# Attention values taken for two query tiles at once, with the column halves' products kept together

## The chip, the cores and the metric

The kernel runs on one core of one Trainium2 chip. The metric is device time in microseconds for one execution of the whole program. Work on a core is done by five engines that run beside each other and meet at semaphores: TensorE (PE; the profile shows its weight loads apart, as PEld), VectorE (DVE), ScalarE (ACT), GpSimd (POOL) and SyncE (SP), which only issues transfers here.

## The reference, cut to what matters

Two layers of a transformer trunk over 512 latent tokens and 256 context tokens, model width 1024, all in fp32. Layer 0 has differential attention (4 heads of width 128) beside neighbourhood attention (8 heads of width 64); layer 1 has windowed attention with 16 query heads of width 64 over 4 key heads. In each the probabilities meet the values at the end, and that product is what the change touches:

```python
# layer 0, differential heads: two softmaxes are subtracted, then times v (width 128)
p = p[:, :, 0] - lam_val * p[:, :, 1]
return jnp.einsum('bhqn,bnhd->bqhd', p.astype(v.dtype), v)
...
# layer 0, neighbourhood heads: keys near the query, and all context keys, in one softmax
return (jnp.einsum('bhcij,bicjhd->bchd', p_nb, v_r)
        + jnp.einsum('bhcn,bnhd->bchd', p_ctx, vcx))
...
# layer 1: a query block of 128 sees the context and the key blocks before, at and after it
band = ... & (jnp.abs(q_pos[:, None] - k_pos[None, :]) <= SWA_WINDOW)
p = jax.nn.softmax(jnp.concatenate([s, sink], axis=-1), axis=-1)[..., :-1]
o = jnp.einsum('bkgqn,bnkd->bqkgd', p.astype(v.dtype), v)
```

Around this stand adaLN-modulated norms, projections with gated residual adds, and a SwiGLU block in each layer.

## The kernel before, in words

Activations lie with features on the partitions and tokens along the free axis, in tiles of 128 features. Most products with weights are made of three fp32r products of split operands (`mm3`, L205 to L210); transposes and the product of probabilities with values are plain fp32.

**A step of attention** handles one tile of 128 queries for one *unit*: one differential head (`diff_steps`, L788), or two heads of width 64 (`na_steps`, L885; `gqa_step`, L1462). A step has two parts. Part `a` makes the scores (L804 and L805, L912 and L914, L1477 and L1479), adds masks and takes the maximum on DVE (L806, L915, L1481), the exponential on ACT (L808, L922, L1486), and normalises on POOL (L782, L926, L1494). Part `b` turns the probabilities on PE, 128 by 128 at a time, into a PSUM tile `t` (L821, L935, L1503, L1511), copies them to SBUF as `pt` (L822 on ACT; L940 on ACT and L938 on DVE; L1507 and L1512 on ACT, L1505 on DVE), multiplies them with the value tiles (L825, L946, L1517), and copies the result out (L826, L949; `split` at L1521, which is L196 on ACT and L197 on DVE). Each context unit has a step of its own (`ca`, `cb`) for its 256 context queries, with products of 256 columns already (L852, L982).

**Column halves.** In units of two heads, the value tile of one head has 64 columns. Head 0 writes PSUM partitions 0 to 63 and head 1 partitions 64 to 127, so each product occupies 64 of the array's 128 columns (the profile prints `128*64`). The loop is over key tiles, and inside it over the two heads.

**Buffers.** `pt` has 3 buffers in layer 0 (`pt_tile`, L785) and 2 in layer 1 (L1499), each for one step (one head of one step in `na_steps`). PSUM tiles `t` take 2 buffers in layer 0 and 3 in layer 1, shared by turned probabilities and products.

**What sets the order.** `run_steps` (L406) writes part `a` of a step, part `b` of the step before, then pieces of other work (projections of the next unit, rows of the adaLN weights, first parts of the output projection). From this the framework's list scheduler makes each engine's fixed order when the kernel is built; it may put an instruction ahead of others whose operands come later, so products of one tile need not stand together. `issue_after` ties an instruction behind another, and `high_priority` puts it ahead of others that are ready.

Of the kernel before, what the change touches and what calls it, by code (L numbers as in the profile page):

```python
# [37 lines left out]
def tile_trunk(  # L38
# [337 lines left out]
    def rope_of(ps, pool, t=None):  # L376
# [7 lines left out]
        return t  # L384

# [209 lines left out]
    with ExitStack() as st:  # L595
# [189 lines left out]
        def pt_tile(n):  # L785
            return ap.tile([P, n, P], F32, tag="pt", name="pt", bufs=3)

        def diff_steps(u):  # L788
# [4 lines left out]
            def x_step(i):  # L793
# [21 lines left out]
                def b():  # L815
                    v = vunits[u // 2]
                    pt = pt_tile(6)
                    for k0, n in ((0, 4), (4, 2)):
                        t = tp((P, 4, P))
                        for k in range(n):  # L820
                            nc.tensor.transpose(t[:, k, :], d["p"][:, (k0 + k) * P : (k0 + k + 1) * P], ident)  # L821
                        nc.scalar.copy(pt[:, k0 : k0 + n, :], t[:, 0:n, :])  # L822
                    o = tp()
                    for k in range(6):
                        nc.tensor.matmul(o[:, 0:P], v[:, k, vc], pt[:, k, :], start=(k == 0), stop=(k == 5))  # L825
                    nc.scalar.copy(at[:, NC + i * P : NC + (i + 1) * P], o[:, 0:P])  # L826
# [58 lines left out]
        def na_steps(u):  # L885
# [5 lines left out]
            def x_step(j):  # L891
# [37 lines left out]
                def b():  # L929
                    v = vunits[u // 2]  # L930
                    pts = []
                    for c in range(2):
                        t = tp((P, 4, P))
                        for k in range(4):
                            nc.tensor.transpose(t[:, k, :], d["p"][c][:, k * P : (k + 1) * P], ident)  # L935
                        pt = pt_tile(4)
                        if c:
                            nc.vector.tensor_copy(pt, t)  # L938
                        else:
                            nc.scalar.copy(pt, t)  # L940
                        pts.append(pt)
                    o = tp()
                    kts = ((2, 5) if j == 0 else (1 + j, 2 + j)) + (0, 1)
                    for k in range(4):
                        for c in range(2):
                            nc.tensor.matmul(  # L946
                                o[64 * c : 64 * c + 64, 0:P], v[:, kts[(k + 2 * c) % 4], hv[c]], pts[c][:, k, :], start=(k == 0), stop=(k == 3)
                            )
                    nc.scalar.copy(at[:, NC + j * P : NC + (j + 1) * P], o[:, 0:P])  # L949
# [15 lines left out]
            def cb():  # L965
                v = vunits[u // 2]
                pts = []
                for c in range(2):
# [4 lines left out]
                    pt = pt_tile(4).rearrange("p (a b) c -> p a (b c)", b=2)  # L973
                    if c:
                        nc.vector.tensor_copy(pt, t)
                    else:
                        nc.scalar.copy(pt, t)
                    pts.append(pt)
                o = tp()
                for k in range(2):  # L980
                    for c in range(2):
# [922 lines left out]
```

## Time and profile before

| what | value |
|---|---|
| median of 3 runs | 1631.01 us (1628.07 to 1631.24) |
| profiled execution, its own time | 1634.54 us |
| its span, first to last instruction | 1632.7 us |
| mean granted TensorE clock | 0.992 |
| TensorE busy | 1569.6 us (96%) |
| VectorE busy | 1255.6 us (77%) |
| ScalarE busy | 747.0 us (46%) |
| GpSimd busy | 267.0 us (16%) |

The program runs in stages one behind the other. By the first and last starts of their lines: differential attention's products with values from 97.7 to 284.7 us (its first scores at 79.7), neighbourhood attention's from 302.9 to 449.5, layer 0's SwiGLU from 557.7, layer 1's attention from 1059.2 (scores) and 1073.6 (products with values) to 1243.4, and layer 1's SwiGLU to the end.

How to read the rows in this document: a timeline row gives the start in us, the length in us, the engine, the line, the operation, `out<-in`, the shape and how many records were merged. A plain fp32 product shows as two MATMUL records for one instruction, a transpose as one. A record's length includes the depth of the array and overlaps its successor, so that the *difference of two starts* is what work costs TensorE.

### The profile page before, as it was taken

The page shows a single profiled execution, that of the slowest core. Times are in us where ns is not written, and L with a number is a line of the kernel's source. Part 1 is how long each engine was busy: PE and PEld are TensorE (multiplying, and loading weights), DVE is VectorE, ACT ScalarE, POOL GpSimd, SP SyncE. Part 2 cuts the span into 40 slices and gives each one's busy share as a digit, 9 for nine tenths or more (in the row PEclk, how much of TensorE's full clock was granted, in tenths as well). Part 3 has the DMA queues.
Part 4 walks back from the last instruction along what each step waited for, and adds up shares of the span by engine and source line. Part 5 has one row for each costly group of instructions (what it writes and reads, how often), then busy time and mean ns, then how long its engine had stood idle before and what let it go on. Part 6 is the DMA issues. An engine that isn't in the chain of part 4 may idle for free.

```text
span 1632.7 us, 26333 instructions
## 1 busy us (share of the span) xinstructions
PE 1569.6 (96%) x10222; PEld 1403.5 (86%) x10222; DVE 1255.6 (77%) x2157; ACT 747.0 (46%) x1324; POOL 267.0 (16%) x311
## 2 busy tenths in 40 slices
PE   5899998998999999999999999999999999999997
PEld 3798887886878899999999998887788899989897
DVE  4757698976688888978899867787665887869686
ACT  4446554555334532432424244456655542524344
POOL 2222222345010000010100011264322000000001
PEclk9999999999999999999999999999999999999999
DMA  9322244544235365576766753311010442323321
GB/s 343 98 57 85 89 149 129 186 139 132 72 109 154 95 183 158 152 197 168 195 180 169 211 134 95 104 53 40 14 40 27 152 132 66 125 82 104 117 78 52
DMA packets 69220, 198.48 MB, mean 122 GB/s; under 512 B 6900, under 2 KB 19348, under 8 KB 69096
## 3 DMA queue, kind: packets, MB, share of 16 engines
q1 hardware_dynamic: 59464, 164.40, 31.7%
q0 software_dynamic: 9056, 31.87, 9.1%
q8 instruction: 81, 1.33, 0.3%
q10 hardware_dynamic: 576, 0.52, 0.1%
q14 instruction: 43, 0.35, 0.1%
HBM read 160.45 MB, written 4.86 MB: 101 GB/s over the span
## 4 chain that ended last, share of the span: by engine, by line
PE 64%; DVE 7%; DMA 4%; issue 2%; ACT 2%; POOL 0%; DVEq 0%; SPq 0%; ACTq 0%; POOLq 0%
PE f L1272 5%; PE f L1274 5%; PE f L1273 5%; PE f L1685 4%; PE f L1684 4%; PE f L1683 4%; PE f L1313 3%; PE f L1314 3%; PE f L1315 3%; PE t L1517 2%; PE lin L207 2%; PE lin L208 2%; PE lin L209 2%; PE f L1737 2%; PE f L1736 2%; PE f L1738 2%
## 5 line engine op out<-in xcount | busy, mean ns | idle before, releaser
L196 ACT ACTIVATE wh<-raw 128x1024 fp32r<-128x1024 f32 (+1 forms) x96 | 92.3, 978 | 233.7 <-DVE raw L507 115.8
L207 PE MATMUL lin<-hb,wh 128*128 128x512 f32 (+1 forms) x456 | 162.8, 358 | 8.2 <-DVE q L372 2.2
L208 PE MATMUL lin<-hb,wh 128*128 128x512 f32 (+1 forms) x456 | 160.3, 352 | 0.5 <-DVE hb L197 0.4
L209 PE MATMUL lin<-hb,wl 128*128 128x512 f32 (+1 forms) x456 | 158.9, 348 | 0.0
L197 DVE TENSOR_TENSOR wl<-raw,wh 128x1024 fp32r<-128x1024 f32 (+1 forms) x96 | 106.8, 1119 | 34.9 <-ACT wh L196 32.9
L269 DVE SCALAR_TENSOR_TENSOR junk<-raw,tables 128x1024 bf16<-128x1024 f32 x80 | 97.7, 1222 | 20.2 <-DMA raw<-in_ada_wT_dram 19.9
L202 POOL DMA_DIRECT2D wl<-raw x39 | 34.1, 873 | 444.1 <-ACT wl L201 393.8
L207 PEld LDWEIGHTS lin<-hb,wh 128*128 128x128 f32 x456 | 86.4, 190 | 23.4 <-issue 4.5
L1313 PE MATMUL f<-g,wh 128*128 128x512 f32 (+1 forms) x304 | 102.8, 339 | 1.2 <-DVE q L1298 0.7
L1314 PE MATMUL f<-g,wh 128*128 128x512 f32 (+1 forms) x304 | 102.7, 339 | 0.0
L1684 PE MATMUL f<-hb,wh 128*128 128x256 f32 x360 | 101.7, 283 | 0.0
L1683 PE MATMUL f<-hb,wh 128*128 128x256 f32 x360 | 101.4, 283 | 0.0
L1685 PE MATMUL f<-hb,wl 128*128 128x256 f32 x360 | 101.2, 283 | 0.0
L1315 PE MATMUL f<-g,wl 128*128 128x256 f32 (+1 forms) x304 | 100.8, 336 | 0.0
L158 ACT CAST wh<-raw 128x1024 fp32r<-128x1024 f32 x61 | 63.9, 1047 | 77.9 <-PE lin L208 24.0
L1272 PE MATMUL f<-hb,wh 128*128 128x384 f32 x288 | 96.4, 335 | 0.9 <-ACT q L1259 0.9
L159 DVE TENSOR_TENSOR wl<-raw,wh 128x1024 fp32r<-128x1024 f32 x61 | 79.8, 1309 | 22.6 <-ACT wh L158 22.4
L208 PEld LDWEIGHTS lin<-hb,wh 128*128 128x128 f32 x456 | 86.7, 190 | 12.2 <-issue 0.9
L1274 PE MATMUL f<-hb,wl 128*128 128x384 f32 x288 | 96.3, 334 | 0.0
L1273 PE MATMUL f<-hb,wh 128*128 128x384 f32 x288 | 96.2, 334 | 0.0
L209 PEld LDWEIGHTS lin<-hb,wl 128*128 128x128 f32 x456 | 86.6, 190 | 10.4 <-issue 0.3
L339 POOL TENSOR_TENSOR ns_a<-ns_a,ns_s 128x256 f32<-128x256 f32 (+1 forms) x16 | 16.2, 1013 | 435.2 <-ACT ns_s L335 435.2
(395 smaller groups left out, 4948.7 us busy)
## 6 DMA issues: line engine op xcount, KB each, us to landing
raw<-in_w_dram SPq DMA_DIRECT2D x132, 512.0 KB, 3.7
raw<-in_ada_wT_dram SPq DMA_DIRECT2D x80, 512.0 KB, 4.2
wl<-raw POOLq DMA_DIRECT2D x39, 512.0 KB, 5.9
raw<-in_w_ab_dram SPq DMA_DIRECT2D x24, 512.0 KB, 4.2
raw<-in_ada_w_dram SPq DMA_DIRECT2D x16, 512.0 KB, 9.5
k<-k SPq DMA_DIRECT2D x16, 384.0 KB, 5.8
raw<-in_w_c_dram SPq DMA_DIRECT2D x12, 512.0 KB, 3.6
nb<-in_na_bias_dram POOLq DMA_DIRECT2D x16, 256.0 KB, 3.6
```

Of the source, the lines that this page charges most:

```text
L207: nc.tensor.matmul(ps, wh(k), xh(k), start=k == 0, stop=False)
L208: nc.tensor.matmul(ps, wh(k), xl(k), start=False, stop=False)
L209: end = nc.tensor.matmul(ps, wl(k), xh(k), start=False, stop=k == n - 1)
L1272: nc.tensor.matmul(ps, wh(k), b[:, 0, :], start=k == 0, stop=False)
L1273: nc.tensor.matmul(ps, wh(k), b[:, 1, :], start=False, stop=False)
L1274: nc.tensor.matmul(ps, wl(k), b[:, 0, :], start=False, stop=k == 3)
L1313: nc.tensor.matmul(ps, hi, g[:, 0, cols[v]], start=first, stop=False)
L1314: nc.tensor.matmul(ps, hi, g[:, 1, cols[v]], start=False, stop=False)
L1315: nc.tensor.matmul(ps, lo, g[:, 0, cols[v]], start=False, stop=last)
L1683: nc.tensor.matmul(ps, wh(k), b[:, 0, :], start=k == 0, stop=False)
L1684: nc.tensor.matmul(ps, wh(k), b[:, 1, :], start=False, stop=False)
L1685: nc.tensor.matmul(ps, wl(k), b[:, 0, :], start=False, stop=k == 3)
```

## The change

1. `diff_steps`: the step of an even query tile only turns its probabilities and copies them into one half of a `pt` of two steps. The step of the odd tile fills the other half and makes six products of 256 columns (two query tiles at once), and one copy of 256 columns out.
2. `na_steps` and `gqa_step`: the same for pairs of query tiles (0, 1) and (2, 3). Key tiles that both tiles see are met in one product of 256 columns, the others in one of 128, which writes only its tile's half of the output.
3. The products of both heads go through the new `values`, which writes them key tile by key tile, head 1 ahead of head 0, and ties each behind the one before with `issue_after` and `high_priority` (`unbroken`). The context steps of `na_steps` go through it too.
4. `pt` has 1 buffer in both layers, of up to 2 x 2 x 4 (layer 0) or 2 x 10 (layer 1) tiles of 128 columns. A norm's scratch tile `ns_h`, which shared the tag `pt`, shares the tag `p` (5 buffers) instead.

```diff
+    def unbroken(products):
+        last = None
+        for f in products:
+            with tc.issue_after(last.ins) if last else nullcontext(), tc.high_priority() if last else nullcontext():
+                last = f()
+
+    def values(o, terms):
+        unbroken([
+            lambda n=n, c=c, v=v, p=p, cols=cols: nc.tensor.matmul(
+                (lambda z: z if len(p(c).shape) == 2 else z.rearrange("p (a n) -> p a n", n=P))(o[64 * c : 64 * c + 64, cols]),
+                v(c), p(c), start=n == 0, stop=n == len(terms) - 1,
+            )
+            for n, (v, p, cols) in enumerate(terms)
+            for c in (1, 0)
+        ])
...
-        def pt_tile(n):
-            return ap.tile([P, n, P], F32, tag="pt", name="pt", bufs=3)
+        def pt_tile(*n):
+            return ap.tile([P, *n, P], F32, tag="pt", name="pt", bufs=1)
...
                 def b():
                     v = vunits[u // 2]
-                    pt = pt_tile(6)
+                    if i % 2 == 0:
+                        turned["d"] = pt_tile(2, 6)
+                    pt = turned["d"]
...
+                    if i % 2 == 0:
+                        return
                     o = tp()
                     for k in range(6):
-                        nc.tensor.matmul(o[:, 0:P], v[:, k, vc], pt[:, k, :], start=(k == 0), stop=(k == 5))
-                    nc.scalar.copy(at[:, NC + i * P : NC + (i + 1) * P], o[:, 0:P])
+                        nc.tensor.matmul(o[:, 0 : 2 * P].rearrange("p (a n) -> p a n", a=2), v[:, k, vc], pt[:, :, k, :], start=(k == 0), stop=(k == 5))
+                    nc.scalar.copy(at[:, NC + (i - 1) * P : NC + (i + 1) * P], o[:, 0 : 2 * P])
...
-                    kts = ((2, 5) if j == 0 else (1 + j, 2 + j)) + (0, 1)
-                    for k in range(4):
-                        for c in range(2):
-                            nc.tensor.matmul(
-                                o[64 * c : 64 * c + 64, 0:P], v[:, kts[(k + 2 * c) % 4], hv[c]], pts[c][:, k, :], start=(k == 0), stop=(k == 3)
-                            )
-                    nc.scalar.copy(at[:, NC + j * P : NC + (j + 1) * P], o[:, 0:P])
+                    values(o, [
+                        term(0, slice(2, 8, 4), both),
+                        term(2 + (j - 2) % 4, 0, slice(0, P)),
+                        term(1 + j, slice(1, 5, 3), both),
+                        term(2 + j, 5, slice(P, 2 * P)),
+                        term(1, slice(3, 8, 4), both),
+                    ])
+                    nc.scalar.copy(at[:, NC + (j - 1) * P : NC + (j + 1) * P], o[:, both])
...
-                for k in range(2):
-                    for c in range(2):
-                        nc.tensor.matmul(o[64 * c : 64 * c + 64, 0:256], v[:, k, hv[c]], pts[c][:, k, :], start=(k == 0), stop=(k == 1))
+                values(o, [(lambda c, k=k: v[:, k, hv[c]], lambda c, k=k: pts[:, c, k, :], slice(0, NC)) for k in range(2)])
...
-            ns_a0=(ap, "at", 2), ns_a1=(ap, "at", 2), ns_s=(ap, "p", 5), ns_h=(ap, "pt", 3),
+            ns_a0=(ap, "at", 2), ns_a1=(ap, "at", 2), ns_s=(ap, "p", 5), ns_h=(ap, "p", 5),
...
-                pt = gp.tile([P, 2, 5, P], F32, tag="pt", name="pt", bufs=2)
+                h = i % 2
+                if h == 0:
+                    turned[0] = gp.tile([P, 2, 10, P], F32, tag="pt", name="pt", bufs=1)
+                pt = turned[0]
...
+                if h == 0:
+                    return
...
-                split(*(z[:, i // 2, P * (i % 2) : P * (i % 2) + P] for z in att(m)), o[:, 0:P])
+                values(o, [
+                    term(0, slice(0, 6, 5), both),
+                    *([term(i, 2, slice(0, P))] if i > 1 else []),
+                    term(1 + i, slice(3, 8, 4), both),
+                    term(2 + i, slice(4, 9, 4), both),
+                    *([term(3 + i, 9, slice(P, 2 * P))] if i < 3 else []),
+                    term(1, slice(1, 7, 5), both),
+                ])
+                split(*(z[:, i // 2, :] for z in att(m)), o[:, both])
```

Over the whole program the instructions of TensorE in the written order go from 9557 to 9333. Only these products differ in number: in the column halves 432 products (416 of 128 columns, 16 of 256) become 256 (64 of 128 columns, 192 of 256), and with full columns 96 of 128 columns become 48 of 256. ACT issues 32 instructions fewer and DVE 16 fewer (the copies out). POOL and SP issue as many as before, and the transfers keep their sizes.

Where it moves instructions, two places on TensorE. Names that begin with `s` are scores, `t<-ident,p` is a turn of probabilities `p`, and `t<-pt` is a product with values. First layer 1's attention. Before, where the products of three steps meet the next steps' scores and turns:

```order
L1503 MATMUL t_10762<-ident_91,p_10693 128x128 x4
L1511 MATMUL t_10768<-ident_91,p_10684 128x128
L1511 MATMUL t_10768<-ident_91,p_10693 128x128
L1517 MATMUL t_10772<-pt_10755,gv_9570 64x128
L1477 MATMUL s_10888<-gk1_9568,gq_10323 128x256
L1477 MATMUL s_10888<-gk2_9569,gq_10323 128x256
L1479 MATMUL s_10888<-gk1_9568,gq_10323 128x384
L1479 MATMUL s_10888<-gk2_9569,gq_10323 128x384
L1517 MATMUL t_10772<-pt_10755,gv_9570 64x128 x7
L1503 MATMUL t_10811<-ident_91,p_10739 128x128 x4
L1517 MATMUL t_10772<-pt_10755,gv_9570 64x128 x2
L1503 MATMUL t_10817<-ident_91,p_10748 128x128 x4
```

The ten products of one step stand in three places: one, seven and two. After the change, a pair of steps in the same stage:

```order
L1542 MATMUL t_10799<-ident_91,p_10741 128x128 x4
L1542 MATMUL t_10805<-ident_91,p_10750 128x128 x4
L1513 MATMUL s_10878<-gk1_9404,gq_10269 128x256
L1513 MATMUL s_10878<-gk2_9405,gq_10269 128x256
L1515 MATMUL s_10878<-gk1_9404,gq_10269 128x384
L1515 MATMUL s_10878<-gk2_9405,gq_10269 128x384
L396 MATMUL t_10811<-pt_10757,gv_9406 64x256 x2
L396 MATMUL t_10811<-pt_10757,gv_9406 64x128 x2
L396 MATMUL t_10811<-pt_10757,gv_9406 64x256 x6
```

Ten products serve two steps and stand in one place, behind the turns of the second step and four score products.

Second, a context step of neighbourhood attention, before:

```order
L972 MATMUL t_3155<-ident_91,pc_2933 128x128 x4
L209 MATMUL lin_3610<-hb7_131,wl_3518 128x256
L982 MATMUL t_3162<-pt_3153,v_1948 64x256
L912 MATMUL s_3415<-k1_2601,q_2603 128x256
L912 MATMUL s_3415<-k2_2602,q_2603 128x256
L914 MATMUL s_3415<-k1_2601,q_2603 128x256
L914 MATMUL s_3415<-k2_2602,q_2603 128x256
L982 MATMUL t_3162<-pt_3160,v_1948 64x256
L982 MATMUL t_3162<-pt_3153,v_1948 64x256
L982 MATMUL t_3162<-pt_3160,v_1948 64x256
```

and the first one after the change:

```order
L209 MATMUL lin_3463<-hb6_130,wl_3401 128x512
L396 MATMUL t_3067<-pt_3054,v_1903 64x256 x4
L964 MATMUL t_3169<-ident_91,p_3047 128x128 x4
```

Its four products stand together, followed at once by the turns of the next step's probabilities. Over the whole order, runs of products in the column halves that stand together number 102 before (64 in layer 1, 38 in neighbourhood attention) and 31 after (18 and 13).

55 lines of the change are left out of this document (31 added, 24 removed).

## The prediction

> **What bounds the kernel now.** I read the page's busy shares first, then the busy time of each engine in the stages that change, then what TensorE waits for there.
>
> ```profile
> span 1632.7 us, 26333 instructions
> PE 1569.6 (96%) x10222; PEld 1403.5 (86%) x10222; DVE 1255.6 (77%) x2157; ACT 747.0 (46%) x1324; POOL 267.0 (16%) x311
> ```
> ```profile
> core 0: us, PE busy (x) PEld busy (x) DVE busy (x) ACT busy (x) POOL busy (x), PEclk, DMA share, GB/s
> 97.00:300.00 203.00, 193.34 (x1325) 176.52 (x1324) 158.07 (x267) 107.42 (x238) 48.54 (x49) 0.98 0.35 106
> 300.00:350.00 50.00, 50.00 (x357) 42.06 (x355) 44.81 (x82) 23.98 (x54) 22.15 (x28) 1.00 0.63 192
> 300.00:450.00 150.00, 144.10 (x1007) 117.97 (x1006) 104.55 (x188) 72.70 (x168) 53.63 (x78) 0.99 0.43 128
> 1067.00:1245.00 178.00, 174.33 (x1344) 138.93 (x1343) 124.24 (x298) 107.54 (x288) 69.40 (x76) 1.00 0.10 31
> ```
> ```profile
> PE t L1517 <- DVE pt L1505: 1.6, 3, 0.8
> PE s L1477 <- ACT p L1486: 1.2, 2, 0.7
> PE t L1517 <- ACT pt L1507: 0.3, 1, 0.3
> ```
>
> The three stages of the windows are differential attention (97 to 300), neighbourhood attention (300 to 450, its first third shown apart) and layer 1's attention (1067 to 1245). In the last, TensorE is idle for 3.7 of 178 us, DVE for 54 and ACT for 70; the longest waits of TensorE on other engines (the wait rows: total, times, longest) come to 3.1 us. In neighbourhood attention it is idle for 5.9 of 150. So TensorE sets the pace in both, at a granted clock of 0.99 to 1.00, and less of its time there means a shorter span. But busy time includes time in which the array passes nothing, and the timeline shows where:
>
> ```profile
> 1152.01 0.60 PE L1503 MATMUL t<-ident,p 128*128 128x128 f32 x4
> 1152.37 0.48 PE L1477 MATMUL s<-gk,gq 128*128 128x256 f32 x2
> ...
> 1157.00 0.51 PE L1479 MATMUL s<-gk,gq 128*128 128x384 f32 x2
> 1157.35 0.38 PE L1511 MATMUL t<-ident,p 128*128 128x128 f32 x2
> 1157.71 1.09 PE L1517 MATMUL t<-pt,gv 128*64 128x128 f32 x16
> 1158.74 0.66 PE L1503 MATMUL t<-ident,p 128*128 128x128 f32 x4
> 1159.15 0.48 PE L1477 MATMUL s<-gk,gq 128*128 128x256 f32 x2
> 1159.46 0.52 PE L1479 MATMUL s<-gk,gq 128*128 128x384 f32 x2
> 1159.91 0.44 PE L1517 MATMUL t<-pt,gv 128*64 128x128 f32 x4
> 1160.28 0.66 PE L1503 MATMUL t<-ident,p 128*128 128x128 f32 x4
> 1160.69 0.48 PE L1477 MATMUL s<-gk,gq 128*128 128x256 f32 x2
> 1161.01 0.52 PE L1479 MATMUL s<-gk,gq 128*128 128x384 f32 x2
> 1161.46 0.43 PE L1517 MATMUL t<-pt,gv 128*64 128x128 f32 x2
> 1161.82 0.66 PE L1503 MATMUL t<-ident,p 128*128 128x128 f32 x4
> 1162.41 1.09 PE L1517 MATMUL t<-pt,gv 128*64 128x128 f32 x14
> 1163.42 0.66 PE L1503 MATMUL t<-ident,p 128*128 128x128 f32 x4
> ```
>
> Call a run of column-half products that stand together a *visit*. I take differences of starts. The visit of 16 records lasts 1.03 us until the next start, that of 4 records 0.37. The 12 records more cost 0.66; two records, one of each half, run side by side, so this is six steps of **0.11 us**. That leaves 0.37 - 2 x 0.11 = 0.15 us in a visit that is no streaming. Ahead of it, the two L1479 records take 0.45 (1161.01 to 1161.46) against 0.35 where a turn follows (1157.00 to 1157.35): 0.10 more. Behind it, four turns and the next take 0.41 (1158.74 to 1159.15) against 0.36 elsewhere (1152.01 to 1152.37): 0.05 more. **A visit costs 0.30 us beside its products.**
>
> The visit of 2 records, one product of one head alone, lasts 0.36: as much as a pair. That of 14 lasts 1.01, nearly the 1.03 of 16. A product without its partner costs a whole pair's time.
>
> **The change part by part.** *Visits.* TensorE's written order has 102 visits before, 64 in layer 1 and 38 in neighbourhood attention, and 31 after, 18 and 13. 71 fewer at 0.30 us are 21.3 us.
>
> *Steps.* I count two steps of 0.11 for each pair of products, and for a product alone too. Layer 1 before has visits of 1, 7, 2, 8 and 10 products (17, 17, 15, 14, 1 of them): 34 + 136 + 30 + 112 + 10 = 322 steps, 35.4 us. After, each of 16 pairs of query tiles has four pairs of products of 256 columns and one of 128. For 256 columns there is a row, with rows of full columns beside it:
>
> ```profile
> 399.16 1.08 PE L982 MATMUL t<-pt,v 128*64 128x256 f32 x8
> 400.18 0.62 PE L207 MATMUL lin<-hb,wh 128*128 128x512 f32 x2
> ...
> 206.45 1.50 PE L825 MATMUL t<-pt,v 128*128 128x128 f32 x12
> 207.79 0.60 PE L821 MATMUL t<-ident,p 128*128 128x128 f32 x4
> ...
> 188.79 1.03 PE L852 MATMUL t<-pt,v 128*128 128x256 f32 x4
> 189.47 0.47 PE L401 MATMUL lin<-wl,hb 128*128 128x256 f32 x1
> ```
>
> Eight records in 1.02 us, less 0.15, are four steps of **0.22**: twice the columns, twice the time. So 16 x (8 x 0.22 + 2 x 0.11) = 31.7 us, and 0.4 for the one visit of a lone product that is left: 3.3 us saved. Neighbourhood attention before: visits of 1, 7, 8, 4 and 3 products (14, 13, 2, 1, 1) are 156 steps, 17.2 us; its context visits (three of 1, three of 3, one of 4) 22 steps of 0.22, 4.8 us. After: 8 x (6 x 0.22 + 4 x 0.11) + 0.4 + 16 x 0.22 = 18.0 us: 4.0 us saved.
>
> *Full columns.* 12 records take 1.34 us, 0.112 each. The 96 records of 256 columns that replace 192 cost between 0.17 (0.68 over four, L852) and 0.224 each, a gain between 5 and 0 us. I take 0.5, since the column halves show time in proportion to columns. TensorE sheds 21.3 + 3.3 + 4.0 + 0.5 = **29.1 us**.
>
> *What comes back.* The products of a pair now wait for the last copy of its second step; before, the first product began behind the first copy, and scores filled the gap. Queued behind the waiting product on TensorE are the next turns and scores, and DVE's maxima and ACT's exponentials wait for these.
>
> ```profile
> L1505 DVE COPY pt<-t 128x512 f32<-128x512 f32 x32 | 22.0, 687 | 11.7 <-PE t L1503 11.6
> L1507 ACT COPY pt<-t 128x512 f32<-128x512 f32 x32 | 18.7, 583 | 7.4 <-PE t L1503 7.1
> L1517 PEld LDWEIGHTS t<-pt,gv 128*64 128x64 f32 x576 | 34.0, 136 | 16.8 <-issue 6.2 <-DVE pt L1505 3.0 <-ACT es L1488 1.4
> L949 ACT COPY at<-t 128x128 f32<-128x128 f32 x16 | 4.3, 266 | 19.6 <-PE t L946 19.3
> ```
>
> The cover in the new order is typically four score products, two lines of two records; such a group takes 0.77 us (1160.69 to 1161.46). Four turns that start 0.11 apart end 0.66 after the first start, so the last ends 0.33 after its own; with DVE's copy its probabilities are there 1.02 us after that start, and the cover has run out after 0.11 + 0.77 = 0.88. So 0.14 us stays bare at least, more where the copy queues. The bounds are 0 a visit, where more stands between, and a whole copy, 0.69, at each of 28 (31 less three broken ones): 0 to 19 us. I take an estimate of 0.25 a visit, **7 us**, nearest the group row. The present 1.9 us of such waits are not credited against it.
>
> *The rest costs nothing.* DVE and ACT issue 16 and 32 copies out fewer (266 ns each, L949), for wider ones, off TensorE's path. A result that waits for its pair is needed a stage later by the output projection; the last pair of the stage alone has no cover, the 1.02 us above, which lies within the bounds. `ns_h` in the five buffers of `p` is covered by the norm's own chain of DVE and ACT; if not, each of eight tiles would wait one DVE instruction. POOL's and SP's queues issue what they did.
>
> *The sum.* 1634.54 (the profiled execution) - 29.1 + 7 = 1612.4 us, a span near 1610.6. The median shown stands at 1631.01 / 1634.54 = 0.9978 of that execution: **1609 us**.
>
> **A rule weighed.** The Trainium skill, "TensorEngine Tiling (Array Packing)", section "PSUM Bottleneck", says that tiling speeds up TensorE but not the emptying of PSUM, so that the copies may become the bound. In this trace DVE works 70% and ACT 60% of layer 1's attention, which leaves room. By the rule the third rival below would hold. The skill's "TensorE: Matmul & The Clock Gate", section "Back-to-back issue gap", gives about 81 ns for a sustained matmul of 128 columns and 131 for 512, which speaks for the second rival; L982 does not agree.
>
> **The rivals.**
>
> *Nothing comes back.* Scores and fillers cover every copy. Then 1605.4 profiled, 1602. For it: waits of only 1.9 us on `pt` now. Against: the cover must now outlast one full copy.
>
> *Weight loads set the step.* If a step were bound by its load (136 ns a record, two per 0.11 us, in the PEld row) and not by its columns, 256 columns would cost 0.136, not 0.22. 16 x 8 + 8 x 6 = 176 new steps would save 14.8 us more than the forecast: 1594. Against: eight records of L982 in 1.02 us.
>
> *The copies become the bound.* DVE's 124.2 us in the last window must fit in some 161 and its 104.6 in about 139: 77% and 75%, and it is at 90% from 300 to 350 us. If each of the 28 visits waits for a whole copy, 19.3 us come back: 1624.7 profiled, **1621**.
>
> *One buffer of `pt` stops the pipeline (slower).* A refill's first copy must wait for the last product that reads the buffer; with two `t` tiles in layer 0 the next turns then wait too. There are 12 refills in each attention of layer 0 (two pairs and the context step, four units) and 16 in layer 1: 40. Were an ACT and a DVE copy (0.58 + 0.69) bare at each, 51 us come back: 1656.5 profiled, **1653**. It decides from 29.1 / 40 = 0.73 us a refill. Against: in the new order the next turns stand behind the products on TensorE anyway, so a copy that waits for its turn finds the buffer free.
>
> *The change doesn't do what it says.* Visits that stand together in the order may run broken by waits, or DVE's pace from 300 to 350 us spreads over its stage, and the time is as before: 1630. Against: TensorE's order is fixed, and 1517's 576 records ran in exactly the written visits.
>
> **How the numbers follow.** Forecast 0.65 (own range 1605 to 1616: 0.1 to 0.5 us bare a visit); nothing comes back 0.12; loads set the step 0.03; the copies bind 0.09; no change 0.05; slower 0.06. Faster by over 0.2% (what a measurement of this kernel tells from no change) is 0.65 + 0.12 + 0.03 + 0.09 = 0.89. The range of 8 in 10 runs from just under the full saving to just past the bound of the copies: 1600 to 1624; it leaves out the loads, no change, slower and the edges.
>
> **What would show it.** In the profile after: 31 visits with 0.30 us each beside their products; a pair's ten products of layer 1 in 8 x 0.22 + 2 x 0.11 + 0.15 = 2.1 us from first start to next start; layer 1's attention shorter by 17.1 us less its waits (46 visits x 0.30 + 3.3), neighbourhood attention by 11.5 less its own (25 x 0.30 + 4.0); TensorE's waits on the `pt` copies risen from 1.9 us to about 7 in all; differential attention as long as now. Wrong would be: waits on `pt` above 19 us, TensorE idle between a visit and the next turns (the one buffer), or the 256-column steps at a time other than 0.22.

## The result

The changed kernel takes **1615.01 us** (median of 4, 1613.67 to 1615.6) against 1630.59 (median of 4, 1628.07 to 1631.24) for the kernel before on the same chip: 0.9906 of it, 95% interval 0.9889 to 0.9923. It is 15.6 us faster; the prediction was 22 us, 1609, with a range from 1600 to 1624. The profiled execution has a span of 1611.6 us against 1632.7. Executions of one kernel scatter by some 4 us to either side, so the 21.1 us between two single spans say less than the medians.

The page of the changed kernel, its span and its busy time:

```profile
span 1611.6 us, 25394 instructions
PE 1538.8 (95%) x9774; PEld 1378.4 (86%) x9774; DVE 1252.2 (78%) x2141; ACT 743.4 (46%) x1292; POOL 273.5 (17%) x311
```

TensorE has 30.8 us less to do (1569.6 before) and the span is 21 us shorter: part of the saving went into idle time. The busy time by stage, in the columns shown for the kernel before, says where:

```profile
core 0: us, PE busy (x) PEld busy (x) DVE busy (x) ACT busy (x) POOL busy (x), PEclk, DMA share, GB/s
97.00:290.00 193.00, 188.13 (x1235) 171.08 (x1234) 157.34 (x268) 109.18 (x236) 51.73 (x52) 1.00 0.36 111
290.00:440.00 150.00, 137.84 (x920) 115.46 (x919) 104.16 (x188) 71.09 (x159) 52.36 (x75) 0.97 0.41 128
1055.00:1222.00 167.00, 157.00 (x1074) 124.50 (x1073) 121.22 (x281) 105.75 (x272) 71.16 (x76) 1.00 0.10 33
```

In layer 1's attention (last row) TensorE is now idle for 10.0 of 167 us; it was 3.7 of 178. What it waits for there, in all, how often, and the longest:

```profile
PE s L1513 <- ACT p L1522: 6.1, 9, 1.3
PE t L396 <- DVE pt L1548: 1.7, 3, 0.9
PE t L1542 <- POOL p L1530: 1.4, 1, 1.4
PE lin L207 <- DVE rt L381: 0.5, 1, 0.5
```

The products' waits for the copies into `pt` (second row) are as short as before, 1.7 us against 1.6 + 0.3. What has grown is the first row: scores that wait until an exponential has emptied a score buffer, 6.1 us against 1.2.

TensorE's timeline shows the visits themselves, first in layer 1, then in neighbourhood attention (a row's own start, and the start of what follows):

```profile
1189.86 2.17 PE L396 MATMUL t<-pt,gv 128*64 128x256 f32 x20
1191.96 1.09 PE L1542 MATMUL t<-ident,p 128*128 128x128 f32 x8
...
1219.27 2.17 PE L396 MATMUL t<-pt,gv 128*64 128x256 f32 x20 [0.88 <-DVE pt L1548]
1221.37 0.50 PE L207 MATMUL t<-hb,wh 128*128 128x512 f32 x1
...
295.12 1.95 PE L396 MATMUL t<-pt,v 128*64 128x256 f32 x20
297.00 0.66 PE L964 MATMUL t<-ident,p 128*128 128x128 f32 x4
```

A pair's ten products of layer 1 take 2.10 us, in neighbourhood attention 1.88. The trace has 31 such visits, as many as the written order.

**The accounts of both stages.** I added up the starts of TensorE's records. *Visits* are the time from a visit's first start to the next start behind it, with what the product ahead of it took beyond its streaming (the usual distance to the next start for its shape); a *gap* is what any other product takes beyond its streaming, if it is over 0.09 us.

| us of TensorE | before | after | change |
|---|---|---|---|
| layer 1, visits and the way into them | 56.1 | 38.1 | -18.0 |
| layer 1, gaps | 8.9 | 18.9 | +10.0 |
| neighbourhood, visits and the way into them (before: mean of two executions) | 33.5 | 23.7 | -9.8 |
| layer 0's attention, gaps (before: two executions, after: the changed kernel and the one with head 0 first) | 32 to 35 | 33 to 36 | about 0 |

The last row hides two things that cancel. TensorE's waits for the keys of a unit, which DVE rotates (L372) and a transfer moves (`k<-k`), grew. Over layer 0's attention, first before, then after:

```profile
PE s L912 <- DMA k<-k: 2.3, 2, 1.6
PE s L805 <- DMA k<-k: 1.7, 1, 1.7
PE lin L207 <- DVE k L372: 0.3, 1, 0.3
```
```profile
PE s L937 <- DMA k<-k: 6.9, 2, 4.2
PE lin L207 <- DVE k L372: 4.2, 2, 3.2
```

Against that, differential attention's products with values take 19.7 us of TensorE from their starts to the next ones, and took 22.9: at the usual times of undisturbed runs of these products the wider ones save only 0.5 of it, and the rest is waits inside and behind them that are gone.

### The profile page after: what moved, and what is told of

It is laid out like the page before. It is cut to its first block, busy times and chain, and to the rows that moved or that the text cites. A ratio compares the mean times of both kernels' runs of the same rounds, so it can differ in the third digit from the quotient of the medians.

```text
span 1611.6 us, 25394 instructions
## 1 busy us (share of the span) xinstructions
PE 1538.8 (95%) x9774; PEld 1378.4 (86%) x9774; DVE 1252.2 (78%) x2141; ACT 743.4 (46%) x1292; POOL 273.5 (17%) x311
## 4 chain that ended last, share of the span: by engine, by line
PE 49%; DVE 10%; DMA 6%; issue 4%; ACT 1%; POOL 0%; DVEq 0%; POOLq 0%; ACTq 0%; SPq 0%
PE f L1737 4%; PE f L1736 4%; PE f L1735 4%; DMA wl<-raw 3%; PE f L208 3%; PE f L209 3%; PE f L207 3%; PE f L1307 2%; PE f L1305 2%; PE f L1306 2%; PE f L1788 2%; PE f L1789 2%; PE f L1790 2%; PE t L396 2%; DMA raw<-in_w_dram 2%
## 5 line engine op out<-in xcount | busy, mean ns | idle before, releaser
L209 PEld LDWEIGHTS lin<-hb,wl 128*128 128x128 f32 x456 | 86.6, 190 | 10.7
L159 DVE TENSOR_TENSOR wl<-raw,wh 128x1024 fp32r<-128x1024 f32 x61 | 79.1, 1297 | 18.0 <-ACT wh L158 17.6
```

Source lines behind the costliest of these rows:

```text
L209: end = nc.tensor.matmul(ps, wl(k), xh(k), start=False, stop=k == n - 1)
```

## The experiments

Twelve kernels ran. Ratios are to the kernel before on the same chip. Kernels that ran on different chips are compared by these ratios alone.

### The kernel before once more

No edit; it shows how far a ratio can be off where nothing differs.

> The kernel of before, unchanged, for a second profile. Theory A: the profiled execution of before (1634.54 us) was 4 us above the median of its other runs (1630.59) because of something that happened in that one execution; then a second profile comes near 1630.6, and one stage is some 4 us shorter than in the first. Rival B: a profile of this kernel always costs that much, and it comes near 1634.5 again with the same stage lengths (attention of layer 0 ending at 449.5, layer 1's from 1059.2 to 1243.4).

Measured: 1629.94 us, ratio 0.9999 (0.9984 to 1.0014). The second profiled execution took 1631.64 us by its own time. From the first to the last visit neighbourhood attention took 142.9 us in it, against 146.6 in the first, so the first was some 4 us long in that one stage, as the first theory had it.

### Each layer alone

One kernel takes the new `gqa_step` and `values` and leaves layer 0 as it was, the other the reverse:

```diff
 # layer 1 only: diff_steps, na_steps, pt_tile, ns_h as before; gqa_step and values of the change
 # layer 0 only: gqa_step as before; diff_steps, na_steps, pt_tile, ns_h, values of the change
```

> The change in layer 1's attention alone (layer 0 as before). The prediction's terms: 46 visits fewer x 0.30 + 3.3 = 17.1 us less of TensorE, 4 us of it given back to copies: 13 us faster, 1617.5. Theory that the scores' two PSUM buffers have become the bound there (TensorE waited 6.1 us on the exponential in the changed kernel, 1.2 before): the stage gets 10 us shorter as in the changed kernel's trace, 1620.5. If layer 0 alone had made the gain: 1630.

> The change in layer 0 alone (layer 1 as before). The prediction's terms: 25 visits x 0.30 + 4.0 + 0.5 = 12 us less, 3 us given back: 9 us faster, 1621.6. By the traces the attention of layer 0 ended 15.7 us earlier, and 3.3 us of that were lost in layer 0's SwiGLU: 1618 if the first profile of before was typical, 1622 if it was 4 us slow in layer 0. If the gains of both layers add up, this and the layer-1 run together save 15.6 us.

Measured: layer 1 alone 1620.92 us, ratio 0.9944 (0.9924 to 0.9964); layer 0 alone 1620.10, 0.9940 (0.9921 to 0.9960). Each is worth some 10 us: what the changed kernel's own trace let expect (1620.5, and 1618 to 1622), and less in layer 1 than the prediction's terms (1617.5). Their product, 0.9884, is not told apart from the 0.9906 of both. From layer 1's first score to the end, the three executions with the old layer 1 take 561.8 to 562.7 us, the two with the new one 553.4 and 553.8: 8.5 us less, and it repeats. The waits for score buffers repeat too: with layer 1 alone they are again 6.1 us in 9 waits. From the first score of differential attention to the last product of neighbourhood attention, four executions with the old layer 0 (this study's other runs taken in) have 365 to 370 us, nine with the new 354.5 to 359.3: 11 us less.

### Head 0's products first, without ties

```diff
-            with tc.issue_after(last.ins) if last else nullcontext(), tc.high_priority() if last else nullcontext():
-                last = f()
+            last = f()
...
-            for c in (1, 0)
+            for c in (0, 1)
```

> Pairs of query tiles as in the change, but head 0's product ahead of head 1's and no ties between products. The written order has 52 visits to the column halves where the changed kernel has 31, and in 17 of them the first product (256 columns) stands alone. Visit theory (0.30 us a visit, a lone product costs a whole pair's two steps of 0.22): 21 x 0.30 + 17 x 0.44 = 13.8 us slower than the changed kernel less what the earlier first product covers, 1624 to 1629. Rival, that the wide products alone make the gain and visits cost nothing that matters: within 2 us of the changed kernel, 1613 to 1617.

Measured: 1620.20 us, ratio 0.9938 (0.9921 to 0.9956); the written order has 52 visits. In layer 1 there are 30 visits and not 18, and 44.1 us of them and the way into them, not 38.1: 6.0 us for twelve visits more, some of them a lone product. The stage gives back part of it in gaps (16.6 against 18.9). The whole is 5.2 us slower than the changed kernel by the ratios, less than the visits' price alone had it (1624 to 1629) and more than the rival (1613 to 1617): in layer 0 no loss shows (354.5 us from the first score to the last product, against 355.9).

Which of the two edits did it can be read from the written orders: the changed kernel without its ties, but with head 1 first, has the same order on every engine, row for row; with head 0 first the ties leave 53 visits. Head 0's probabilities are copied on ACT and are there before head 1's, which DVE copies. With head 0 first the scheduler can place its first product early, alone; with head 1 first nothing can start before the later copy. It is the order of the two heads that keeps the products together, and `issue_after` and `high_priority` add nothing here.

### The price of a visit

Both kernels add one product of a tile of zeros with all 128 columns to each of the 28 lists of products (the results stay what they are); in one it stands behind the first pair and cuts the visit, in the other behind the last product:

```diff
-        unbroken([
+        fs = [
...
-        ])
+        ]
+        fs.insert(2, lambda: nc.tensor.matmul(o[:, 0:P], ident, none, start=False, stop=False))
+        unbroken(fs)
```

(`fs.insert(len(fs), ...)` in the second, where it is also the product that ends the sum.)

> Added work: after the first pair of products of every visit stands one product of a tile of zeros over all 128 columns of the array (128 columns wide, added to the same result, which it leaves as it is). It cuts 29 of the 31 visits in two. Theory: a visit costs 0.30 us beside its products. The zero products are 31 x 2 records x 0.112 = 6.9 us, the 29 visits more are 8.7 us: about 1615.0 + 15.6 = 1630.6, and 8.7 us above the kernel that has the same zero products behind its visits; down to 5 us above it where TensorE would have been idle anyway. Rival (a change of column mode is free, the gain came from fewer steps and from another order): the same time as that kernel, within 2 us.

> The same zero products, each as the last product of its visit, so that a visit stays whole (32 visits) and its way back to full columns lies between the products and the zero product. Theory and rival alike: 1615.0 + 6.9 = 1621.9, less where TensorE would have been idle (down to 1618). It is there to be set against the kernel that has them inside.

Measured: 1625.85 us with the product inside (ratio 0.9959, 0.9944 to 0.9974; the trace has 60 visits), 1618.92 with it behind (0.9920, 0.9897 to 0.9943; 32 visits). The difference is 6.9 us for 28 visits, 0.25 each (5 to 8.7 us were forecast), and the timelines have the price itself. With the product inside:

```profile
1190.92 0.65 PE L396 MATMUL t<-pt,gv 128*64 128x256 f32 x4
1191.50 0.49 PE L403 MATMUL t<-gm,ident 128*128 128x128 f32 x2
1191.92 1.73 PE L396 MATMUL t<-pt,gv 128*64 128x256 f32 x16
1193.59 1.09 PE L1544 MATMUL t<-ident,p 128*128 128x128 f32 x8
```

With it behind:

```profile
1195.24 2.17 PE L396 MATMUL t<-pt,gv 128*64 128x256 f32 x20
1197.34 0.49 PE L403 MATMUL t<-gm,ident 128*128 128x128 f32 x2
1197.66 1.04 PE L1544 MATMUL t<-ident,p 128*128 128x128 f32 x8
```

The same 22 records take 2.67 us until the turns start in the first and 2.42 in the second, and the eight turns behind take 0.05 more in the first: 0.30 us for one visit more, as the prediction priced it. The rival, that a change of column mode is free, falls. (The Trainium skill's "TensorEngine Tiling (Array Packing)", section "Key Properties", says that changing the tiling mode drains TensorE; the trace agrees, at 0.30 us a visit.)

The second kernel holds a surprise. Its 16 zero products in layer 1 take 0.24 to 0.33 us each to the next start, 4.7 us in all, and two visits more 0.6; from layer 1's first score to TensorE's last product it takes 560.8 us against 553.8. The added work did **not** go into TensorE's idle time, which is 10.7 of the 174.4 us of layer 1's attention in the changed kernel and 10.8 of 181.1 here. But not all of the 7.0 us is added work, since one stretch of this trace runs at half the clock:

```profile
1111.00:1117.60 6.60, 5.64 (x24) 4.45 (x25) 4.41 (x13) 3.07 (x8) 3.87 (x5) 0.50 0.25 79
```

5.64 us of products at a granted clock of 0.50 are, by my estimate, 2.8 us more than at 1.00, which the changed kernel has in the whole stage. So some 4 us remain for 5.3 us of added work: most of it is paid. In neighbourhood attention no cost shows: 137.8 us from the first to the last visit, where the changed kernel has 138.7 and five other executions of its layer 0 have 136.6 to 140.4.

### Where layer 1's gaps come from: four trials

The theory after these runs: in layer 1 the linear products that fill TensorE's time run out, and a step without them is bound by the chain from scores to the maximum (DVE), the exponential (ACT) and the next score's buffer. The first trial lets the linear products take their PSUM from the ring of the turns; the scheduler then spreads them. The second does the same with a third score buffer.

```diff
-        lin = st.enter_context(tc.tile_pool(name="g_lin", bufs=1, space=PSUM, reuse_waits="tile"))
-        tps = st.enter_context(tc.tile_pool(name="g_t", bufs=3, space=PSUM, reuse_waits="tile"))
+        tps = st.enter_context(tc.tile_pool(name="g_t", bufs=4, space=PSUM, reuse_waits="tile"))
...
-        linp = lambda: lin.tile([P, NX], F32, tag="lin", name="lin")
+        linp = lambda: tps.tile([P, NX], F32, tag="t", name="t")
```

(In the second: `bufs=3` for the scores `g_s`, `bufs=2` for `g_t`.)

> In layer 1's attention the linear products that fill TensorE's time (queries of later heads, first parts of the output projection) take their PSUM from the ring of the turns (4 buffers) and not from a buffer of their own. In TensorE's written order they then stand spread over the whole stage (groups of 24 or 12 records every few steps) and not at its two ends; 34 visits, 31 before. Theory (the 10 us of idle time in layer 1 are steps without fillers, bound by the chain from score to maximum to exponential to the next score's buffer): the idle time goes down by 4 to 8 us, 1607 to 1611, with the waits on score buffers down from 6.1 us. Rival (products wait for the copies into the one probability buffer): nothing that decides is changed, and three visits are added: 1615 to 1616.

> As the run with spread fillers, with a third PSUM buffer for layer 1's scores, paid for with two buffers of the turns (2 and not 4); 31 visits. Theory (two score buffers hold the step up): waits on score buffers nearly gone, 4 to 8 us less than the changed kernel, 1607 to 1611, and if fewer buffers for turns cost, back to 1613. Rival (copies of the turned probabilities decide): with two buffers for turns the copies are felt sooner, so slower than the changed kernel, 1617 to 1625.

Measured: 1659.3 us, ratio 1.0173 (1.0144 to 1.0202), and 1657.14, ratio 1.0147 (1.0121 to 1.0172). Every forecast missed by more than 30 us. Of the first kernel, the waits of TensorE for score buffers, one stretch of 50 us, a visit behind it, and the stretch of that visit:

```profile
PE s L1512 <- ACT p L1521: 26.7, 20, 3.5
...
1050.00:1100.00 50.00, 40.65 (x223) 32.50 (x223) 30.01 (x70) 26.20 (x67) 19.51 (x21) 0.84 0.11 32
...
1110.32 3.85 PE L396 MATMUL t<-pt,gv 128*64 128x256 f32 x20 [2.45 <-DVE pt L1547]
...
1110.30:1114.20 3.90, 3.88 (x21) 2.60 (x21) 1.61 (x4) 2.16 (x7) 1.36 (x2) 0.56 0.21 83
```

With its own buffer, a linear product's 24 records are laced with scores and turns. In the shared ring they stand in one run of 5.5 us, during which DVE and ACT get next to nothing to do (0.4 us each of the 5.6 us from 1114.1); behind it TensorE waits for them. After such waits the granted clock is down (0.84 in the stretch of 50 us, 1.00 in the changed kernel's layer 1): from 1049 to 1267 us it falls to 0.50 seven times, 37 us in all, each time with 2.0 to 3.4 us of waiting in the 5 us ahead. The visit that begins after 2.45 us of waiting stands in such a stretch, 0.56 on average, and takes 3.85 us, not 2.17. With three score buffers the waits for them are still 18.1 us. These two runs therefore don't test the number of score buffers: both carry the long runs of linear products.

The next pair keeps the linear products' own buffer and ties them in the written order behind the steps' scores, in groups of 6, in the changed kernel and, as a control, in the kernel before.

```diff
+                for k in range(KT * i // n, KT * (i + 1) // n):      # part i of n of a query tile's product
+                    with tc.issue_after(mark[0].ins):                # mark: the step's last score
+                        nc.tensor.matmul(ps, wh(k), xh(k), start=k == 0, stop=False)
...
-            fillers += spread(plan[m], 4)
+        for m in range(2, 8):
+            for i, f in enumerate(q_parts(m, 4)):
+                fillers[4 * m - 6 + i].append(f)
+        for n, f in zip((23, 25, 26, 27, 28, 29, 30, 31), firsts):
+            fillers[n].append(f)
```

> The changed kernel with the linear products of layer 1's attention (the query tiles of later heads, the first parts of the output projection) held back in TensorE's order: each head's 24 come in four groups of 6, one group behind each step's scores, and the first parts one group of 12 a step near the end. They keep their own PSUM buffer. Nothing is added or left out; 33 visits, 31 before. Theory (the 10 us more of idle time arise because these products and the query tiles' work on DVE stand in clumps: where they are bunched DVE and ACT wait for TensorE, behind them TensorE waits for DVE and ACT): the gaps of layer 1's attention go down from 18.9 us by 4 to 8, so 1607 to 1611. Rival (the chain from score to maximum to exponential to the next score sets the step, whatever stands between): 1615, within 2 us. If groups hold up the scores as the clumps of 24 did: above 1620.

> The same holding back in the kernel before the change (98 visits in all, 102 before), as a control. Theory: the kernel before has 8.9 us of gaps in layer 1's attention, half of what the changed kernel has, so there is little to win: 1627 to 1631. Rival (spreading is worth the same in both): as much faster as the changed kernel gets.

Measured: 1625.08 us, ratio 0.9953 (0.9938 to 0.9969), and 1641.31, ratio 1.0054 (1.0035 to 1.0073). (In both, the last query tile's product and a first part of the output projection are under way at once in the one buffer, so that these two are mixed; the amount of work is as described.) Spreading made both kernels slower, by 7 to 9 us. Most of that is one wait of my own making, at the stage's first score:

```profile
1052.30 0.80 PE L1532 MATMUL s<-gk,gq 128*128 128x256 f32 x2 [5.85 <-DVE gq L372]
```

The tie holds head 1's 24 records behind the first scores, while in the changed kernel they fill TensorE's time until head 0's query tile is ready. Beside that, the gaps of the changed kernel from the ninth step of layer 1 on fell from 15.8 to 10.9 us, and those of the first eight rose from 3.0 to 10.9. The sum, 21.8 against 18.8, did not fall; but two stretches among the first eight steps, 9.3 us together, ran at a granted clock of 0.50, the first right behind that wait, and I estimate half of the 7.8 us of products in them, 3.9 us, as their price. The trial does not show that another placing wins the gaps back; one that leaves the first tile where it was has not run.

The last of the four makes ACT's part of the chain shorter:

```diff
-                    nc.scalar.activation(es[:, c : c + 1], snk[:, sk : sk + 1], AF.Exp, bias=mx[:, c : c + 1], scale=-1.0)
                     pp.append(p)
+                nc.vector.tensor_sub(es, mx, snk[:, 2 * m : 2 * m + 2])
+                nc.scalar.activation(es, es, AF.Exp)
```

> The changed kernel, with the exponential of the sink computed once a step for both heads (DVE subtracts, 128x2; ACT one exponential, 128x2) and not once a head behind each score's exponential: 0.29 us less on ACT a step, 0.16 us more on DVE. 30 visits. Theory of the score chain on ACT (a score buffer comes free late because ACT is behind): some 16 steps without cover at 0.2 to 0.3 us, 3 to 5 us less: 1610 to 1612. Theory of clumps (DVE holds it up there, at 9.1 of 10 us): no gain, 1615 to 1617.

Measured: 1619.87 us, ratio 0.9918 (0.9892 to 0.9944): no gain over 0.9906. The waits for score buffers:

```profile
PE s L1513 <- ACT p L1522: 6.5, 8, 1.6
```

6.5 us against 6.1, and the stage's gaps 21.5 against 18.9, with 10 us (1113.5 to 1123.5) at a granted clock of 0.50 among them, so that the waits compare better than the gaps. The wait is put down to ACT's exponential, but 0.37 us less on ACT a step (the exponentials of the sinks took 18.2 us in 32 steps, and 6.5 here) did not shorten it. ACT was itself waiting: in the changed kernel's 10 us from 1103, 2.3 us for DVE's maxima. Where the largest gaps lie, DVE is what is full. Two stretches of the changed kernel:

```profile
1091.00:1103.00 12.00, 11.99 (x73) 9.28 (x70) 7.16 (x15) 5.05 (x13) 4.17 (x4) 1.00 0.15 45
1103.00:1113.00 10.00, 6.26 (x37) 4.75 (x37) 9.13 (x22) 7.23 (x18) 4.47 (x4) 1.00 0.09 22
```

and TensorE in the second:

```profile
1106.31 0.50 PE L1513 MATMUL s<-gk,gq 128*128 128x256 f32 x2 [0.53 <-ACT p L1522]
...
1108.38 0.50 PE L1513 MATMUL s<-gk,gq 128*128 128x256 f32 x2 [1.33 <-ACT p L1522]
...
1112.64 1.32 PE L1542 MATMUL t<-ident,p 128*128 128x128 f32 x8 [1.39 <-POOL p L1530]
```

For 12 us TensorE runs linear products and a visit without a pause, and DVE works 7.2 us of them. DVE's next maximum waits 5.2 us for its score, which stands behind that visit. Then the maxima, the copies, the rotation of a query tile (L380, L381, L372) and the split of a weight tile (L159) come together: DVE works 9.1 of 10 us and TensorE 6.3. A full DVE alone does not stop TensorE. In the kernel before it works 11.7 of the 12 us of one stretch, and TensorE, which had 35 linear records there, 11.8:

```profile
1090.00:1102.00 12.00, 11.82 (x65) 9.77 (x64) 11.68 (x21) 6.45 (x17) 9.60 (x8) 1.00 0.15 45
```

In the kernel before, the third group of four steps, in which the changed kernel's stretch lies, had 30 linear records left to cover it; now 9, since the scheduler put the others into the second group (69 for 49). That group's gaps rose from 0.8 to 6.0 us, half of the 10; another 3.1 are in the last group, ahead of which 24 linear records were left and not 37.

### Products of one half behind each other

```diff
-            for n, (v, p, cols) in enumerate(terms)
             for c in (1, 0)
+            for n, (v, p, cols) in enumerate(terms)
```

> The changed kernel, with all products of a visit for the second head first and then all of the first head, so that two products that stand together lie in the same column half; 36 visits. Nothing else is changed. Theory (products of the two halves run side by side, and a product alone takes a pair's whole time): a visit's steps double, so the 31.7 + 18.0 us of steps come once more, about 49 us, less what idle time takes up: 1655 to 1664. Rival (each half's products stream one after the other in any case, and 0.11 us is the time of two): 1615 to 1618.

Measured: 1639.31 us, ratio 1.0052 (1.0034 to 1.0069): some 24 us above the changed kernel, neither of the two forecasts. A visit of ten products and one of four (context) in neighbourhood attention:

```profile
297.88 3.08 PE L396 MATMUL t<-pt,v 128*64 128x256 f32 x20
300.90 0.65 PE L964 MATMUL t<-ident,p 128*128 128x128 f32 x4
...
331.96 1.09 PE L396 MATMUL t<-pt,v 128*64 128x256 f32 x8
332.98 0.66 PE L964 MATMUL t<-ident,p 128*128 128x128 f32 x4
```

and the four products in the changed kernel:

```profile
330.82 1.08 PE L396 MATMUL t<-pt,v 128*64 128x256 f32 x8
331.83 0.65 PE L964 MATMUL t<-ident,p 128*128 128x128 f32 x4
```

The ten products take 3.02 us, 1.14 more than the 1.88 of the changed kernel; the four take 1.02, no more than there. The starts of single records say why. In the four, the first product of head 0, third in the written order, starts 0.014 us behind the very first. In the ten, head 1's first three products run alone, in 1.13 us (by the pairs' times 0.43, 0.22 and 0.43, and 0.05); then head 0's start beside head 1's last two; head 0's last three run alone again. So a product that has no partner takes a whole pair's time, as the prediction had it, and a half with nothing to do starts a product up to two places ahead of its turn. The forecast of 49 us held all five terms of a visit unpaired; it is three of five.

## Why the prediction was right in its range, and 6 us off

**Visits: right.** 0.30 us each was forecast from three rows of one timeline; a visit added by hand costs 0.30. 31 visits stand in the trace.

**Steps and what they shed: right.** 2.10 us for ten products of layer 1 (2.1 forecast); 256 columns take twice the time of 128, so loads don't set the step. Layer 1 shed 18.0 us for 17.1, neighbourhood attention 9.8 for 11.5: 27.8 for the 28.6 of the two. The 0.5 for full columns holds for the wider products themselves (20.2 us at the usual times before, 19.7 after); 2.7 us of waits at these products went with it, which the sum did not have. "Differential attention as long as now" can't be checked: the two attentions of layer 0 overlap, and the saving shows as 11 us on both together.

**What comes back: the failed step.** The term was 7 us: 28 visits at 0.25 us, bare waits for the copies into `pt`, rising from 1.9 us to about 7. In layer 1 these waits are 1.7 us, in neighbourhood attention 2.4. The mechanism named came at six visits alone, 4.1 us in all where such waits were 2.7 before: cover was enough nearly everywhere, as that rival said, and the longest in layer 1 is at the stage's last visit (0.88 us, of the 1.02 forecast). That the time lies in the range is luck as far as this term goes, since the range's upper end was the price of these copies. What did come back is larger, 12.2 us of the 27.8 by the medians, and most of it lies in places that the prediction did not cost:

- *Layer 1, 10.0 us of gaps, where 4 of waits were forecast (16 visits at 0.25).* Scores and turns wait for DVE, ACT and POOL where few linear products are left. The prediction had read 3.7 us of idle TensorE in that stage as "TensorE sets the pace", and the 70% of DVE as room. It was an average: in 1103 to 1113 us DVE is at 91%, and TensorE has few other products left there; where the kernel before had them, TensorE lost 0.2 us of 12 beside a DVE at 97%. Shown are the places and the waits; that the products' moved places cause them is argued from the counts (69 and 9 for 49 and 30). The runs rule out that it is ACT's share alone (the single sink exponential gains nothing), and make it unlikely that idle time there is spare (5.3 us of added work left it at 10.8 us, where it was 10.7). Whether a better placing wins it back stays open.
- *The norm ahead of SwiGLU, 1.3 us, costed at nothing.* The prediction feared that `ns_h` would wait for a buffer of `p`. It is the other way round: with five buffers and not three, DVE scales five tiles in a row before it makes the first low part (L355), for which TensorE's second product waits. First the changed kernel, then the one before:

```profile
472.19 3.39 DVE L353 SCALAR_TENSOR_TENSOR ns_h<-res,amod,ns_y 128x512 f32<-128x512 f32 x5
...
476.30 0.51 PE L208 MATMUL f<-hb,wh 128*128 128x512 f32 x1 [1.59 <-DVE hb L355]
```
```profile
487.68 2.07 DVE L353 SCALAR_TENSOR_TENSOR ns_h<-res,amod,ns_y 128x512 f32<-128x512 f32 x3
...
490.46 0.50 PE L208 MATMUL f<-hb,wh 128*128 128x512 f32 x1 [0.27 <-DVE hb L355]
```

  All ten traces with the new layer 0 have this wait, and none of the four with the old one. From SwiGLU's first product to layer 1's first score the old ones take 575.7 to 577.7 us, the new ones 577.0 to 581.0 (and 582.7 in the spread kernel, whose first score has the wait of 5.85 us); what is beyond 1.3 of that goes with waits for weights at changing places, and is not explained.

The sum by traces: 11 in layer 0 and 8.5 from layer 1 on, less the 1.3 to 3 in SwiGLU, 16.5 to 18; the medians say 15.6, with an interval from 12.6 to 18.1.

**The rivals.** *Nothing comes back* was nearly right on `pt` and wrong on the time. *The copies become the bound* fell in its own terms, with 4.1 us of waits on `pt` in both stages and not 19; the Trainium skill's "TensorEngine Tiling (Array Packing)", section "PSUM Bottleneck", says that the copies out of PSUM may become the bottleneck. The copies of `pt` are not what most of the gaps wait for here; for stretches it is the maxima and other work of DVE, which also copies. *One buffer of `pt`* is refuted: no wait of TensorE, ACT or DVE in the trace is for its reuse, and the time is 38 us below that forecast. (No kernel with two such buffers ran.) *Loads set the step* fell with the 2.10 us.

## What to carry to other kernels

Price a change of array shape by the starts of records, once per place where it switches, and count the places in the written order: over both stages that part came out within a few per cent (27.8 us for 28.6). Then ask, of the engine that is now relieved, in which ten microseconds another one is already full and little else stands in the relieved one's order: a stage's average hides them, and work that filled the gaps moves when the scheduler finds TensorE free earlier. More buffers for a scratch tile are an edit to the order too.

## What the runs showed of the hardware

- The array's column halves take products independently, in these runs up to two places ahead in TensorE's queue: head 0's first product started 0.014 us behind the first of head 1 with another one between them, so that four products in an order that pairs only the middle ones took 1.02 us, as long as in paired order (1.01). Ten products written half by half took 3.02 us, in pairs 1.88.
- A switch to the column halves and back costs 0.30 us beside the products: 0.25 us a visit on the whole kernel (6.9 us for 28), and in one timeline 2.67 us against 2.42, with 0.05 on the turns behind.
- Waits can slow what follows them: after 2.45 us of waiting a visit took 3.85 us where it takes 2.17, with a granted clock of 0.56 in these 3.9 us. Not each such wait was followed by a lower clock (one of 2.33 us, before 1074.6, was not). Such stretches stand in the layer 1 of several of the trials, and have to be read off before their gaps are compared.
